# Scaling the softmax probabilities on GpSimd instead of VectorE, in both attentions of a two-layer hybrid block

## The chip, the cores and the metric

The kernel runs on one core of one Trainium2 chip. The metric is the device time of one execution in microseconds (us). Five engines work side by side, each through its own instructions strictly in the order in which they were written down: TensorE (PE; its weight loads are shown apart as PEld), VectorE (DVE), ScalarE (ACT), GpSimd (POOL) and SyncE (SP), which here only issues the transfers.

## The reference, cut to what matters

Two layers (`DEPTH = 2`), each over 256 tokens x and 256 context tokens of width 1024. Each layer has three branches (neighbourhood attention "NA", a gated spatial MLP, and latent attention "MLA"), gated and merged, then a squared-ReLU MLP. Only layer 0 also updates the context. Both attentions have 8 heads, and both end in the same softmax:

```
s = einsum(q, k) * scale          # NA: + bias, masked to a window
p = softmax(s, axis=-1)
y = einsum(p, v)
```

Queries of x attend to all 512 tokens; queries of the context (layer 0 alone) attend to the 256 context tokens.

## The kernel before, in words

Every projection is written as three matmuls per 128-row step (`mm3`, lines 287 to 289): a weight is split into a high part `wh` (ACT, line 115) and a remainder `wl` (DVE, line 116), and so are the activations.

Both attentions go through `soft_pv`. It takes a pair of heads at a time (`hh`) and 128 queries at a time (`qt`). For each head the steps are:

1. the score matmul into a PSUM tile `S` (tag "s", 2 buffers; line 410/411 in NA, line 417 in MLA)
2. in NA for queries of x, DVE adds the bias (line 443)
3. DVE takes the negated row maximum `nm` (line 445)
4. ACT writes `P = exp(S + nm)` to SBUF (tag "P", 2 buffers) and its row sum `sm` (line 448, two instructions)
5. DVE takes the reciprocal `r` (line 450)
6. DVE multiplies `P` by `r` in place (line 451)
7. PE turns `P` in blocks of 128x128 into a PSUM tile `pt` (tag "pt", **1 buffer**; line 454, four blocks for 512 keys, two for 256)
8. ACT copies `pt` to SBUF as `PT` (line 456)

When both heads and both `qt` are turned, PE multiplies `PT` by the values into `pv` (line 460). So a `pt` block can't start before ACT has copied the one before it, an exponential can't start before the `P` two heads earlier is turned, and a score can't start before the exponential two heads earlier has read its `S`.

While an attention runs, PE also has projection work that needs nothing of it: the gate and `z` matmuls of `merge` (lines 287 to 289). `paced` hands them out: each step of a projection may be issued only after a given score matmul (the `marks`). In layer 0 the projections work on 512 tokens, in layer 1 on 256. There are 96 heads' softmaxes in all: 32 in each attention of layer 0 (16 over 512 keys, 16 over 256) and 16 over 512 keys in each attention of layer 1.

The order of the instructions of each engine is not that of the source: the program is built with `schedule_with_timeline_sim=True`, a scheduler that lays out each engine's list ahead of time from its own estimates of durations. An edit to one operation can so move the others.

Of the kernel before, what the change touches and what calls it, by code (L numbers as in the profile page):

```python
# [10 lines left out]
ALU = mybir.AluOpType  # L11
# [15 lines left out]
def hybrid_block_kernel(tc, a, out):  # L27
    nc = tc.nc
    act = nc.scalar.activation
    vec = nc.vector  # L30
# [3 lines left out]
    with ExitStack() as es:  # L34
# [12 lines left out]
        def psum(tag, name):  # L47
            return pp.tile([128, 512], F32, tag=tag, name=name, bufs={"mm": 4, "s": 2, "pt": 1, "pv": 1}[tag])
# [378 lines left out]
        def soft_pv(score, V, pv, streams, bias, marks):  # L427

            for v in range(streams):
                kts = [0, 1, 2, 3] if v == 0 else [2, 3]  # L430
                k0, nk = kts[0] * 128, 128 * len(kts)
                PT = [gp.tile([128, 4, NX], F32, tag="PT", name="PT", bufs=2) for _ in range(2)]
                for qt in range(2):
                    q0 = v * NX + qt * 128
                    S = []
                    for hh in range(2):
                        s = psum("s", "S")
                        marks.append(score[hh](s[:, :nk], q0, k0, nk).ins)
                        S.append(s)
                    for hh in range(2):  # L440
                        s = S[hh]
                        if bias is not None and v == 0:
                            vec.tensor_tensor(out=s[:, :NX], in0=s[:, :NX], in1=bias[hh][:, qt, :], op=ALU.add)
                        nm = sp.tile([128, 1], F32, tag="nm", name="nm")
                        vec.tensor_reduce(out=nm, in_=s[:, :nk], axis=AX.X, op=ALU.max, negate=True)
                        P = gp.tile([128, 512], F32, tag="P", name="P", bufs=2)
                        sm = sp.tile([128, 1], F32, tag="sm", name="sm")
                        act(out=P[:, :nk], in_=s[:, :nk], func=AF.Exp, bias=nm, accum_out=sm)
                        r = sp.tile([128, 1], F32, tag="r", name="r")
                        vec.reciprocal(r, sm)  # L450
                        vec.tensor_scalar(out=P[:, :nk], in0=P[:, :nk], scalar1=r, scalar2=None, op0=ALU.mult)
                        pt = psum("pt", "pt")
                        for i in range(len(kts)):
                            nc.tensor.transpose(pt[:, i * 128:(i + 1) * 128], P[:, i * 128:(i + 1) * 128], ident)  # L454
                        n = len(kts)
                        turned = act(out=PT[hh][:, :n, qt * 128:(qt + 1) * 128],
                                     in_=pt[:, :nk].rearrange("p (i q) -> p i q", i=n), func=AF.Copy)
                for i, kt in enumerate(kts):
                    for hh in range(2):
                        m = mm(pv[64 * hh:64 * hh + 64, v * NX:(v + 1) * NX], lhsT=V[kt][hh], rhs=PT[hh][:, i, :],  # L460
                               start=(i == 0), stop=(i == len(kts) - 1), tile_position=(0, 64 * hh))
                        if i == 0 and hh == 0:

                            tc.add_manual_dep(m.ins, turned.ins.name, mybir.DependencyInfo(
                                mybir.DependencyClass.Sync, mybir.DependencyReason.DATA), reason="both heads")
# [68 lines left out]
        for l in range(L):  # L534
# [114 lines left out]
            for t in range(4):  # L649
                vec.tensor_scalar(out=cnat[t][:, 0:128], in0=cnat[t][:, 0:128], scalar1=rsc[:, t:t + 1], scalar2=None,  # L650
                                  op0=ALU.mult)
                if t in tts:
                    vec.tensor_scalar(out=cnat[t][:, 160:416], in0=cnat[t][:, 160:416], scalar1=rsc[:, 4 + t:5 + t],
                                      scalar2=None, op0=ALU.mult)
# [72 lines left out]
            for j in range(4):  # L727
                bias = []
                for hh in range(2):
                    bt = gp.tile([128, 2, NX], F32, tag="bias", name="bias", bufs=2)  # L730
                    with tc.issue_after(last_load[0]):
                        nc.sync.dma_start(out=bt, in_=a["nab"][l, 2 * j + hh])
                    bias.append(bt)
                pv = psum("pv", "pv")
                soft_pv([na_score(kT, qT, 2 * j + hh) for hh in range(2)],
                        [[vna[t][:, (2 * j + hh) * 64:(2 * j + hh + 1) * 64] for hh in range(2)] for t in range(4)],
                        pv, ns, bias, marks)
                H, Lo = split_out(pv, "yna", T)
                ynH.append(H)
                ynL.append(Lo)  # L740
# [86 lines left out]
            for j in range(4):  # L827
                pv = psum("pv", "pvm")
                soft_pv([mla_score(kmT, qmT, 2 * j + hh) for hh in range(2)],
                        [[vml[t][:, (2 * j + hh) * 64:(2 * j + hh + 1) * 64] for hh in range(2)] for t in range(4)],  # L830
                        pv, ns, None, marks)
                H, Lo = split_out(pv, "yml", T)
                ymH.append(H)
                ymL.append(Lo)
# [44 lines left out]
            for n in range(both, 8):  # L879
                out_chunk(a["wa"][l, 28 + n], n, mixH, mixL, [0], 16, acc)  # L880
                if last:
# [3 lines left out]
                                             op0=ALU.mult, op1=ALU.subtract)  # L885
# [165 lines left out]
```

## Time and profile before

| what | value |
|---|---|
| median of 3 runs | 1401.68 us (1401.63 to 1404.64) |
| the profiled execution | 1406.83 us, span 1404.8 us |
| PE busy | 1375.1 us (98% of the span) |
| PEld busy | 1165.9 us (83%) |
| DVE busy | 958.2 us (68%) |
| ACT busy | 703.5 us (50%) |
| POOL busy | 58.7 us (4%), 35 instructions |
| mean granted TensorE clock | 0.996 |

Busy time is the sum of an engine's instructions; a matmul's end is modelled, so a busy PE may still be waiting inside a row. The times of rows are counted from the start of the span. The profiled execution's own time is 5.15 us over the median of the runs.

### The profile page before, as it was taken

Reading aid. Unit: us, or ns where it says so; the run is one execution under the profiler, and the core shown is the slowest. Engines: PE = TensorE matmul, PEld = TensorE weight load, DVE = VectorE, ACT = ScalarE, POOL = GpSimd, SP = SyncE. Lnnn points to the kernel's source line nnn. Section 1 sums busy time; section 2 is a strip of 40 time slices with the busy share of each in tenths; the row PEclk is TensorE's granted clock in tenths of the full one; section 3 lists DMA queues with packets and bytes.
Section 4 is the critical chain, followed back from the end, with each engine's and each line's share of the span. In section 5 each row is a group of like instructions: output and inputs, shape, how many; then the busy total and the mean of one; then the engine's idle time right before and its main releaser. Section 6 shows DMA issues by size and latency. Waiting matters only on the chain.

```text
span 1404.8 us, 22573 instructions
## 1 busy us (share of the span) xinstructions
PE 1375.1 (98%) x8438; PEld 1165.9 (83%) x8438; DVE 958.2 (68%) x2071; ACT 703.5 (50%) x1440; POOL 58.7 (4%) x35
## 2 busy tenths in 40 slices
PE   6999999999999999999999999999999999999999
PEld 4888767777677789988888888988878879999998
DVE  4666477665563558899766665786778766877775
ACT  3466256444453346623324233566666665656654
POOL 0110000110000000000000000011003000000000
PEclk9999999999999999999999999999999999999999
DMA  9423542233313455765555552443533425666554
GB/s 335 144 84 105 181 143 90 74 106 120 120 45 106 135 189 169 211 206 173 195 199 192 181 193 90 149 137 94 180 106 110 124 78 166 192 181 177 184 182 149
DMA packets 67213, 210.61 MB, mean 150 GB/s; under 512 B 8608, under 2 KB 9632, under 8 KB 67104
## 3 DMA queue, kind: packets, MB, share of 16 engines
q1 hardware_dynamic: 67104, 209.18, 46.8%
q8 instruction: 66, 1.08, 0.3%
q14 instruction: 43, 0.35, 0.1%
HBM read 208.10 MB, written 1.05 MB: 149 GB/s over the span
## 4 chain that ended last, share of the span: by engine, by line
PE 96%; DVE 2%; ACT 1%; DMA 1%; issue 0%; SPq 0%; POOL 0%; ACTq 0%; DVEq 0%
PE o_ps L287 8%; PE o_ps L289 8%; PE o_ps L288 8%; PE f L288 6%; PE f L289 6%; PE f L287 6%; PE gate L287 5%; PE gate L288 5%; PE gate L289 5%; PE b_ps L287 5%; PE b_ps L288 4%; PE b_ps L289 4%; PE pt L454 3%; PE S L417 2%; PE z L287 2%; PE z L288 2%
## 5 line engine op out<-in xcount | busy, mean ns | idle before, releaser
L115 ACT ACTIVATE wh<-raw 128x512 fp32r<-128x512 f32 (+2 forms) x570 | 352.9, 626 | 517.4 <-PE o_ps L288 189.1
L116 DVE TENSOR_TENSOR wl<-raw,wh 128x512 fp32r<-128x512 f32 (+2 forms) x570 | 386.2, 685 | 185.0 <-ACT wh L115 180.2
L289 PE MATMUL f<-hH,wl 128*128 128x258 f32 (+2 forms) x560 | 180.7, 323 | 0.1
L287 PE MATMUL f<-hH,wh 128*128 128x258 f32 (+2 forms) x560 | 180.2, 323 | 0.5 <-ACT wh L115 0.5
L288 PE MATMUL f<-hL,wh 128*128 128x258 f32 (+2 forms) x560 | 180.3, 323 | 0.2 <-DVE hL L277 0.2
L288 PE MATMUL o_ps<-aL,wh 128*128 128x256 f32 (+1 forms) x544 | 176.0, 327 | 0.0
L287 PE MATMUL o_ps<-aH,wh 128*128 128x256 f32 (+1 forms) x544 | 175.8, 328 | 0.0
L289 PE MATMUL o_ps<-aH,wl 128*128 128x256 f32 (+1 forms) x544 | 175.4, 327 | 0.0
L287 PE MATMUL gate<-hH,wh 128*128 128x512 f32 (+1 forms) x384 | 140.9, 367 | 0.0
L289 PE MATMUL gate<-hH,wl 128*128 128x512 f32 (+1 forms) x384 | 131.4, 342 | 0.0
L288 PE MATMUL gate<-hL,wh 128*128 128x512 f32 (+1 forms) x384 | 131.1, 341 | 0.0
L287 PEld LDWEIGHTS f<-hH,wh 128*128 128x128 f32 x560 | 105.9, 190 | 9.0 <-ACT wh L115 0.7
L289 PEld LDWEIGHTS f<-hH,wl 128*128 128x128 f32 x560 | 106.1, 190 | 8.4 <-DVE wl L116 0.3
L288 PEld LDWEIGHTS f<-hL,wh 128*128 128x128 f32 x560 | 105.8, 190 | 8.7 <-DVE hL L277 0.4
L287 PEld LDWEIGHTS o_ps<-aH,wh 128*128 128x128 f32 x544 | 102.7, 190 | 9.4 <-ACT aH L918 0.8
L288 PEld LDWEIGHTS o_ps<-aL,wh 128*128 128x128 f32 x544 | 103.0, 190 | 8.7
L289 PEld LDWEIGHTS o_ps<-aH,wl 128*128 128x128 f32 x544 | 102.7, 190 | 8.8
L288 PE MATMUL b_ps<-wl,hH 128*128 128x512 f32 (+2 forms) x288 | 108.6, 380 | 0.0
L289 PE MATMUL b_ps<-wh,hL 128*128 128x512 f32 (+2 forms) x288 | 106.2, 380 | 0.0
L287 PE MATMUL b_ps<-wh,hH 128*128 128x512 f32 (+2 forms) x288 | 103.6, 385 | 0.0
L200 DVE SCALAR_TENSOR_TENSOR macc<-rawx,sS,macc 128x512 f32<-128x512 f32 x112 | 79.1, 750 | 28.8 <-DMA rawx<-in_wmod_dram 28.8
L287 PEld LDWEIGHTS gate<-hH,wh 128*128 128x128 f32 x384 | 73.6, 192 | 15.9 <-issue 7.5
(226 smaller groups left out, 2490.1 us busy)
## 6 DMA issues: line engine op xcount, KB each, us to landing
raw<-in_wa_dram SPq DMA_DIRECT2D x147, 512.0 KB, 3.6
raw<-in_w_dram SPq DMA_DIRECT2D x68, 512.0 KB, 3.6
raw<-in_wb_dram SPq DMA_DIRECT2D x32, 512.0 KB, 3.3
raw<-in_wmod_dram SPq DMA_DIRECT2D x32, 512.0 KB, 3.4
rawx<-in_wmod_dram SPq DMA_DIRECT2D x32, 512.0 KB, 4.5
raw<-in_wo_dram SPq DMA_DIRECT2D x24, 512.0 KB, 3.5
rawm<-in_wmod_dram SPq DMA_DIRECT2D x32, 256.0 KB, 6.0
rawx<-in_wmod_dram SPq DMA_DIRECT2D x32, 256.0 KB, 4.1
```

The source lines that it names most:

```text
L115: act(out=wh[:, :width], in_=src, func=AF.Copy)
L116: vec.tensor_tensor(out=wl[:, :width], in0=src, in1=wh[:, :width], op=ALU.subtract)
L200: summed = vec.scalar_tensor_tensor(out=o, in0=src, scalar=s, in1=o, op0=ALU.mult, op1=ALU.add)
L287: mm(ps, lhsT=sh, rhs=mh, start=first, stop=False)
L288: mm(ps, lhsT=sh, rhs=ml, start=False, stop=False)
L289: mm(ps, lhsT=sl, rhs=mh, start=False, stop=last)
L417: return mm(s, lhsT=Q[h][0:96, q0:q0 + 128], rhs=K[h][0:96, k0:k0 + nk], start=True, stop=True)
L454: nc.tensor.transpose(pt[:, i * 128:(i + 1) * 128], P[:, i * 128:(i + 1) * 128], ident)
```

## The change

The multiplication of `P` by `r` (line 451) is issued on GpSimd instead of VectorE. `soft_pv` serves both attentions, so all 96 of these move.

```
-                        vec.tensor_scalar(out=P[:, :nk], in0=P[:, :nk], scalar1=r, scalar2=None, op0=ALU.mult)
+                        nc.gpsimd.tensor_scalar(out=P[:, :nk], in0=P[:, :nk], scalar1=r, scalar2=None, op0=ALU.mult)
```

The scheduler then lays the lists out anew. On POOL the 96 rows stand between the reciprocal square roots (`rsh`) that were there alone. Near the end of layer 0's NA (`ssk` is a sum of squares of the keys that MLA needs):

```order
 L329 TENSOR_TENSOR rsh_2702<-ssk_2699,mhalf_86 128x8
+L451 TENSOR_SCALAR P_2393<-P_2393,r_2396 128x256
 L329 TENSOR_TENSOR rsh_2725<-ssk_2722,mhalf_86 128x8
```

The last of the 32 scalings of this attention now stands behind one such root.

On PE the transpositions move. In layer 1's NA (`P_10171` and `P_10186` are the two heads of one `qt`; `S_10219` and `S_10252` are scores of later ones):

```order
 L288 MATMUL gate_10515<-hL_8398,wh_10509 128x256
 L289 MATMUL gate_10515<-hH_8390,wl_10510 128x256
-L454 MATMUL pt_10177<-ident_79,P_10171 128x128 x4
 L410 MATMUL S_10219<-naK_9465,naQ_9244 128x512
 L411 MATMUL S_10219<-naK_9465,naQL2_9245 128x512
...
 L288 MATMUL z_10542<-yg_10006,wh_10543 128x256
 L289 MATMUL z_10542<-yg_10006,wl_10544 128x256
+L454 MATMUL pt_10177<-ident_79,P_10171 128x128 x4
 L454 MATMUL pt_10192<-ident_79,P_10186 128x128 x4
 L410 MATMUL S_10252<-naK_9462,naQ_9244 128x512
```

Where a score and two steps of `z` (six rows, of which the middle is left out) stood between the two heads' transpositions, the two now stand side by side, with nothing between them.

The same in layer 1's MLA, with a score and four steps of `gate` between the two before:

```order
 L288 MATMUL gate_11693<-hL_8393,wh_11683 128x256
 L289 MATMUL gate_11693<-hH_8385,wl_11684 128x256
-L454 MATMUL pt_11170<-ident_79,P_11164 128x128 x4
 L417 MATMUL S_11222<-kml_10854,qml_11114 128x512
 L287 MATMUL gate_11693<-hH_8386,wh_11683 128x256
...
 L289 MATMUL gate_11693<-hH_8389,wl_11688 128x256
+L454 MATMUL pt_11170<-ident_79,P_11164 128x128 x4
 L454 MATMUL pt_11188<-ident_79,P_11182 128x128 x4
 L417 MATMUL S_11224<-kml_10862,qml_11119 128x512
```

Here too the two transpositions become neighbours. Counted over the whole PE list, such neighbours (a transposition of one head right behind that of another) are:

| attention | before: 512 keys / 256 keys | after: 512 keys / 256 keys |
|---|---|---|
| NA, layer 0 | 1 / 0 | 6 / 2 |
| MLA, layer 0 | 0 / 0 | 4 / 4 |
| NA, layer 1 | 3 / 0 | 7 / 0 |
| MLA, layer 1 | 0 / 0 | 3 / 0 |

One of the three of layer 1 before, and two of the four over 256 keys in MLA of layer 0 after, have one matmul of a projection between the two. The list of SP, which issues the transfers, is the same as before.

## Rows read from the trace of the kernel before

**Rows 1.** The page: busy time of each engine, then the chain that ended last.
```profile
PE 1375.1 (98%) x8438; PEld 1165.9 (83%) x8438; DVE 958.2 (68%) x2071; ACT 703.5 (50%) x1440; POOL 58.7 (4%) x35
...
PE 96%; DVE 2%; ACT 1%; DMA 1%; issue 0%; SPq 0%; POOL 0%; ACTq 0%; DVEq 0%
```
**Rows 2.** Stretches of NA, MLA (layer 0), NA, MLA (layer 1): busy by engine, PEclk, DMA.
```profile
180.00:256.00 76.00, 73.40 (x429) 52.05 (x428) 55.48 (x146) 47.86 (x122) 0.18 (x1) 0.98 0.32 100
334.00:456.00 122.00, 122.00 (x645) 85.47 (x644) 61.86 (x148) 55.06 (x133) 0.00 (x0) 1.00 0.30 95
1013.00:1063.00 50.00, 43.92 (x289) 34.89 (x288) 36.55 (x90) 31.72 (x73) 0.00 (x0) 0.97 0.34 102
1107.00:1168.00 61.00, 60.91 (x430) 49.66 (x430) 38.10 (x82) 36.20 (x81) 0.00 (x0) 1.00 0.29 89
```
**Rows 3.** Steps of the softmax over all 96 heads: ns min/median/max.
```profile
L451 DVE TENSOR_SCALAR P<-P,r x96: 344/480/489, 186.6 to 1158.2; 128x512 f32<-128x512 f32 x64, 128x256 f32<-128x256 f32 x32
L448 ACT ACTIVATE P<-S,nm x96: 467/682/697, 185.6 to 1157.2; 128x512 f32<-128x512 f32 x64, 128x256 f32<-128x256 f32 x32
L456 ACT ACTIVATE PT<-pt x96: 364/597/602, 189.5 to 1163.6; 128x512 f32<-128x512 f32 x64, 128x256 f32<-128x256 f32 x32
```
**Rows 4.** Who waited for a tile P, in total: us, times.
```profile
  PE pt L454: 0.2, 1
```
**Rows 5.** Timeline of PE's weight loads, NA of layer 1: start us, us, ..., [wait before].
```profile
1032.59 0.46 PEld L454 LDWEIGHTS pt<-ident,P 128*128 128x128 f32 x4
1034.04 0.42 PEld L454 LDWEIGHTS pt<-ident,P 128*128 128x128 f32 x4 [0.98 <-ACT PT L456]
1034.70 0.19 PEld L410 LDWEIGHTS S<-naK,naQ 128*128 128x128 f32 x1 [0.25 <-ACT P L448]
...
1036.24 0.46 PEld L454 LDWEIGHTS pt<-ident,P 128*128 128x128 f32 x4
1036.66 0.19 PEld L410 LDWEIGHTS S<-naK,naQ 128*128 128x128 f32 x1
```
**Rows 6.** The same view at two other neighbouring pairs of before (NA).
```profile
209.04 0.59 PEld L454 LDWEIGHTS pt<-ident,P 128*128 128x128 f32 x4
210.61 0.42 PEld L454 LDWEIGHTS pt<-ident,P 128*128 128x128 f32 x4 [0.98 <-ACT PT L456]
211.27 0.19 PEld L410 LDWEIGHTS S<-naK,naQ 128*128 128x128 f32 x1 [0.25 <-ACT P L448]
...
1044.64 0.42 PEld L454 LDWEIGHTS pt<-ident,P 128*128 128x128 f32 x4 [0.82 <-ACT PT L456]
```
**Rows 7.** Timeline of ACT and DVE: the softmax of the head turned at 1036.24.
```profile
1034.45 0.20 ACT L448 ACTIVATION_READ_ACCUMULATOR P<-S,nm 128x1 f32 x1
...
1034.69 0.16 DVE L450 RECIPROCAL r<-sm 128x1 f32<-128x1 f32 x1 [0.67 <-ACT P L448]
1034.96 0.49 DVE L451 TENSOR_SCALAR P<-P,r 128x512 f32<-128x512 f32 x1
```
**Rows 8.** POOL's instructions by form: busy us, mean ns of one.
```profile
L329 POOL TENSOR_TENSOR rsh<-ssk,mhalf 128x8 f32<-128x8 f32 x8 | 14.1, 1784 | 180.1 <-DVE ssk L765 180.1
...
masks.py:199 POOL TENSOR_SCALAR_AFFINE_SELECT ident<-ident 128x128 f32<-128x128 f32 x1 | 0.3, 292 | 0.1
masks.py:197 POOL MEMSET ident<- 128x128 f32 x1 | 0.2, 204 | 0.3 <-POOLq L1040 0.3
...
L1040 POOL MEMSET const-float32-1.0<- 128x1 f32 x1 | 0.1, 98 | 0.0
```
**Rows 9.** Waits of PE's weight loads in NA of layer 1 (1013 to 1063): us, times, longest.
```profile
PEld S L410 <- ACT P L448: 3.4, 5, 1.3
PEld pt L454 <- ACT PT L456: 2.7, 3, 1.0
```
**Rows 10.** A stretch of NA of layer 1 after an idle time of PE; columns as in rows 2.
```profile
1018.60:1021.70 3.10, 3.10 (x15) 3.00 (x14) 2.92 (x7) 1.38 (x4) 0.00 (x0) 0.52 0.27 52
```
**Rows 11.** DVE's remainder `wl` over the whole run: ns min/median/max.
```profile
L116 DVE TENSOR_TENSOR wl<-raw,wh x570: 549/691/715, 20.0 to 1396.2; 128x512 fp32r<-128x512 f32 x182, 128x416 fp32r<-128x416 f32 x6, 128x384 fp32r<-128x384 f32 x2
```

## The prediction
> **What bounds the kernel now.** Read first the page's busy shares and the chain of waits: PE is busy for 98% of the span and carries 96% of the chain that ended last, DVE 2%, ACT 1%, POOL nothing [rows 1]. Whatever doesn't make PE stand still, or spare it a standstill, is worth nothing; DVE, from which the work is taken, is at 68%. Then read the four stretches in which the attentions run [rows 2]. In MLA of layer 0 PE has no idle time (122.00 of 122.00 us), in MLA of layer 1 almost none (60.91 of 61), in NA of layer 0 2.6 us and in NA of layer 1 6.1 us. So the softmax hides behind the projections' matmuls except in NA, and there the waits show what ends last: PE waits for ACT's exponential to give a score tile back (3.4 us) and for ACT's copy to give `pt` back (2.7 us) [rows 9]. For the scaling itself PE waited 0.2 us, once, in the whole run [rows 4]. That one number says that there is nothing to win on the line that is edited.
>
> **Part 1, what leaves DVE.** 64 scalings of 512 columns at 0.48 us and 32 of 256 at 0.344 [rows 3]: 64 x 0.48 + 32 x 0.344 = 41.7 us of DVE. All of it lies beside PE's work [rows 1, 4]. Worth 0.
>
> **Part 2, what POOL gets.** No row of before shows a multiplication on POOL, so it is bounded by its neighbours [rows 8]. Below: filling 128 columns takes 204 ns and one column 98, that is 0.83 ns per column, so 512 columns take 0.53 us. Above: the select over 128 columns takes 292 ns, which over the same 98 ns is 1.53 ns per column, so 0.88 us. [...] I take the upper end, 0.88 (0.49 for 256 columns), as the select reads a tile like the scaling does. The 96 scalings are then 64 x 0.88 + 32 x 0.49 = 72 us on an engine that was busy for 58.7 [rows 1].
>
> Is the longer way to `P` covered? Take the head whose exponential ends at 1034.65 and which is turned at 1036.24 [rows 5, 7]. DVE was done with it at 1035.45, so 0.79 us were to spare. On POOL the scaling takes 0.40 us more and hands over twice between engines; one such step costs some 0.2 us by the row, since ACT's sum ends at 1034.65 and the scaling, after a reciprocal of 0.16 and its own wait, starts at 1034.96. 0.40 + 0.2 is less than 0.79: covered, with the order as it was. In the new order this very head (`P_10171`) is turned a score and two steps of `z` later. Those two things took from 1034.70 to 1036.24 less one step of three matmuls (0.35), 1.2 us. So POOL may take up to about 0.79 + 0.48 + 1.2 - 0.2 = 2.3 us before PE waits for it. Cost 0. Where nothing follows to cover it, at the ends of the two NA stages, and where one root (1.78 us) now stands in front of the last scaling, I put 1.5 us on the path.
>
> **Part 3, what moves on PE.** This is the term that decides. `pt` has one buffer, so the second of two neighbouring transpositions can't start before ACT has copied the first. The rows of before have this case [rows 5]: the first starts at 1032.59, the second, after 0.98 us of waiting for the copy, at 1034.04, and the score behind it, after another 0.25 us for the exponential, at 1034.70: 2.11 us. A transposition that stands alone takes from 1036.24 to 1036.66, 0.42 us. The pair costs 2.11 - 2 x 0.42 = **1.27 us**, and since PE runs in order nothing can fill it. The other pairs agree: waits of 0.98 and 0.82 us, and 2.23 us from start to score for the one in layer 0 [rows 6].
>
> The order has 20 such pairs over 512 keys where it had 4: 16 x 1.27 = 20.3 us. It has 6 over 256 keys where it had none. No row shows one of those; the copy takes 0.364 us there where it takes 0.597 [rows 3], so 1.27 - 0.23 = 1.04, of which I take 1.0 as two of the six still have a matmul in between: 6.0 us. Bounds per pair: 0.82, the smallest wait seen, to 1.39 (2.23 - 0.84) for 512 keys; 0.6 (0.82 - 0.23) to 1.27 for 256.
>
> Against it: a pair does at once some of the waiting that single heads do now. Of the 6.1 us that PE waits in NA of layer 1 for a score tile and for `pt` [rows 9], 3.4 + 2.7, the three pairs of before hold at most 3 x (0.98 + 0.25) = 3.7, and the first score's wait stays; I take off 2 us there and 1.3 us in NA of layer 0. The MLA stages have no such wait to give back [rows 2]. Nothing else changes place: SP's list is the same.
>
> **Sum.** 0 + 0 + 1.5 + 20.3 + 6.0 - 3.3 = +24.5 us. The profiled execution took 1406.83 us and would take 1431.3. It lies 5.15 us over the median of the runs, and the terms are rows of the same kernel, so I put the sum on the median: 1401.68 + 24.5 = **1426.2 us**. Own ends: low 16 x 0.82 + 6 x 0.6 = 16.7, less 5 for waits given back: +12, or 1413.7. High 16 x 1.39 + 6 x 1.27 = 29.9, plus 3 for the ends of stages, plus a lower clock: after the idle time before 1018.6 the granted clock was 0.52 for 3.1 us [rows 10], the lower of its two levels (1.2 GHz), which loses half of 3.1, some 1.6 us; five such more are 8: +41, or 1443. After the pairs of before no fall shows, so the sum has none.
>
> **Rivals.**
> *Faster.* The scaling leaves DVE's list, where it queues behind other work, so `P` could be ready earlier, and the waits for ACT in NA shrink with it. If all that PE waits in NA of layer 1 for score tiles and `pt` went [rows 9], that is 6 us, 1395.6. It decides only if a neighbouring pair costs under about 0.2 us, so that 22 of them stay under 4 us; all rows of pairs show 0.8 us and more, and PE hardly waited for the scaling [rows 4]. 4%.
> *No change.* The pairs' waits stand where PE would have waited anyway. That holds for NA at best; in the MLA stages PE is busy to the end [rows 2]. To bring all of the 24.5 us within the 4.2 us (0.3%) that a measurement can tell from no change, the MLA pairs would have to cost nothing. 5%.
> *Late scaling.* POOL takes over 2.3 us for 512 columns, and PE waits for `P`. For it: POOL's one arithmetic row costs 1.78 us for 8 columns [rows 8], and DVE works on SBUF all the while, `wl` at 0.69 us a piece [rows 11]. Against it: fill and select run at about 1 ns per column. With 3 us each full scaling is 0.7 us late: 64 x 0.7 = 45 on top of 24.5, 1471. 10%.
> The Trainium skill, page "SBUF — State Buffer", section "Who interferes with whom", states that VectorE instructions with two SBUF inputs and GpSimd instructions that read SBUF hold a shared port pair exclusively, and whichever comes second waits for the whole of the other. `wl` has two SBUF inputs. By that rule a scaling could wait out one `wl`: 0.88 + 0.69 = 1.57 us, still under 2.3, so the sum by it stays +24.5; no run here shows it yet.
> That the change doesn't do what it says is out: 96 rows leave DVE's list and 96 come into POOL's.
>
> **How the numbers follow.** 81% for the forecast, 10% for the late scaling, 5% for no change, 4% for faster. Slower by over 0.3%: 81 + 10 = 91%; within 0.3%: 5%; faster: 4%. The range takes the forecast's own ends, goes on below to where two thirds of the sum are given back elsewhere (+8) and above into the milder late scalings (half of that rival's 45 us on top): 1409 to 1449.
>
> **What would show it.** Right: PE's idle time in the four stretches grows by some 20 us in all; waits of `pt` for ACT's copy rise from 5 us or less in the NA stages to about 20, some 0.9 each; DVE loses 42 us; POOL shows 96 scalings under 1 us, and PE hardly waits for `P`. Wrong: pairs with waits of under 0.4 us; PE waiting for POOL; scalings of over 2 us; a lower granted clock that lasts through a stage.

## The result, and the profile after

The changed kernel takes **1438.97 us** (median of 4 runs, 1438.4 to 1440.74), the kernel before beside it on the same chip 1401.66 us: the medians lie **37.3 us** apart, and by all runs together it takes 1.0259 times as long [1.0244, 1.0275]. The forecast was +24.5 us, in a range of +7 to +47. The profiled execution of after took 1438.53 us.

The page of after, the lines that answer to [rows 1]:

```profile
PE 1381.6 (96%) x8438; PEld 1163.0 (81%) x8438; DVE 928.7 (65%) x1975; ACT 704.7 (49%) x1440; POOL 188.6 (13%) x131
...
PE 93%; ACT 2%; DVE 2%; DMA 1%; issue 1%; SPq 0%; POOL 0%; ACTq 0%; DVEq 0%; POOLq 0%
```

DVE lost 96 instructions and 29.5 us, POOL got 96 and 129.9 us. The chain still runs through PE, but ACT now holds 2% of it: PE stands and waits for ACT more than it did.

Where the time went is read from the four stretches in which the attentions run, each from its first score matmul to that of the next, or to POOL's next root behind it. The columns are those of [rows 2]. The kernel before first, in a second profiled execution (why the second, is told under the last experiment):

```profile
182.32:333.18 150.86, 145.47 (x814) 108.88 (x813) 100.48 (x241) 80.15 (x190) 13.64 (x8) 1.00 0.33 104
333.18:537.84 204.66, 204.34 (x1097) 154.85 (x1096) 110.79 (x236) 90.32 (x196) 0.00 (x1) 1.00 0.39 124
1011.40:1105.43 94.03, 87.03 (x625) 76.18 (x623) 74.52 (x177) 62.37 (x139) 13.98 (x6) 0.98 0.40 125
1105.43:1219.46 114.03, 113.99 (x868) 102.29 (x868) 80.15 (x184) 68.52 (x148) 0.00 (x1) 1.00 0.41 131
```

And after:

```profile
180.45:347.35 166.90, 150.61 (x815) 109.96 (x813) 91.88 (x210) 81.95 (x193) 54.41 (x40) 0.99 0.31 94
347.35:560.78 213.43, 207.30 (x1097) 155.46 (x1096) 100.48 (x204) 90.37 (x196) 39.96 (x33) 1.00 0.38 118
1034.35:1133.60 99.25, 88.06 (x624) 75.44 (x622) 69.77 (x161) 61.78 (x139) 37.15 (x22) 0.98 0.38 117
1133.60:1252.96 119.36, 115.83 (x868) 102.42 (x868) 75.60 (x168) 68.67 (x148) 26.17 (x16) 1.00 0.40 125
```

The length of a stretch is its second number, PE's busy time the third. NA of layer 0 is 16.0 us longer, MLA 8.8, NA of layer 1 5.2, MLA 5.3: together 35.4 us of the rows unrounded, and what lies between and behind the stretches has not changed. What lies in front of the first is 1.9 us shorter here (180.45 against 182.32 us), and it differs between the two profiled executions of before as well (181.04 in the first). PE's idle time in the four stretches (length less busy) rose from 5.4 + 0.3 + 7.0 + 0.0 = 12.7 us to 16.3 + 6.1 + 11.2 + 3.5 = 37.1, by 24.4.

What PE waited for over the whole run of after (us, times, longest; PEld are its weight loads, "issue" names nobody):

```profile
PEld pt L454 <- issue: 23.7, 34, 1.0
PE pt L454 <- ACT PT L456: 19.5, 27, 1.0
...
PEld pt L454 <- POOL P L451: 11.0, 12, 1.6
...
PEld S L410 <- ACT P L448: 8.8, 22, 1.4
...
PE pt L454 <- POOL P L451: 2.5, 2, 1.3
```

The same wait for the copy in the second execution of before:

```profile
PE pt L454 <- ACT PT L456: 2.8, 4, 0.7
```

The copy that gives `pt` back costs PE 19.5 us, where it was 2.8 in four waits before. And PE now waits for POOL's scaling, which before was 0.2 us, once [rows 4]. One neighbouring pair in MLA of layer 1 of after, where before PE had no idle time (the timeline of PE, its weight loads and ACT, columns as in [rows 5]):

```profile
1145.17 0.46 PEld L454 LDWEIGHTS pt<-ident,P 128*128 128x128 f32 x4
1145.27 0.60 PE L454 MATMUL pt<-ident,P 128*128 128x128 f32 x4
...
1145.91 0.60 ACT L456 ACTIVATE PT<-pt 128x512 f32<-128x512 f32 x1 [0.93 <-PE pt L454]
...
1146.62 0.42 PEld L454 LDWEIGHTS pt<-ident,P 128*128 128x128 f32 x4 [0.99 <-issue]
1146.65 0.63 PE L454 MATMUL pt<-ident,P 128*128 128x128 f32 x4 [0.78 <-ACT PT L456]
...
1147.22 0.30 PEld L417 LDWEIGHTS S<-kml,qml 96*128 96x128 f32 x2 [0.19 <-ACT P L448]
```

The copy starts at 1145.91 and takes 0.60; only then, at 1146.62, does the second transposition begin. From the first weight load to the score behind the pair it is 2.05 us, 1.21 more than two transpositions that stand alone (0.42 each [rows 5]). That is the pair of [rows 5] over again, in a stage that had none.

The scaling on POOL itself, by form (busy us, mean ns of one, then the idle time before it):

```profile
L451 POOL TENSOR_SCALAR P<-P,r 128x512 f32<-128x512 f32 x64 | 102.2, 1602 | 218.8 <-DVE r L450 208.3 <-PE gate L288 5.0 <-PE mod_ps L137 2.1
L451 POOL TENSOR_SCALAR P<-P,r 128x256 f32<-128x256 f32 x32 | 30.1, 940 | 57.3 <-DVE r L450 46.6 <-PE pt L454 10.5
```

1.60 us where DVE needed 0.48, and 0.94 where it needed 0.344. The forecast had 0.88 and 0.49. From 256 to 512 columns it is 0.66 us more, 2.6 ns a column; the select of [rows 8], which the forecast took for the nearest row, gave 1.53.

### The profile page after: what moved, and what is told of

It is laid out like the page before. It is cut to its first block, busy times and chain, and to the rows that moved or that the text cites. A ratio compares the mean times of both kernels' runs of the same rounds, so it can differ in the third digit from the quotient of the medians.

```text
span 1436.7 us, 22752 instructions
## 1 busy us (share of the span) xinstructions
PE 1381.6 (96%) x8438; PEld 1163.0 (81%) x8438; DVE 928.7 (65%) x1975; ACT 704.7 (49%) x1440; POOL 188.6 (13%) x131
## 4 chain that ended last, share of the span: by engine, by line
PE 93%; ACT 2%; DVE 2%; DMA 1%; issue 1%; SPq 0%; POOL 0%; ACTq 0%; DVEq 0%; POOLq 0%
PE o_ps L287 8%; PE o_ps L289 8%; PE o_ps L288 8%; PE f L288 6%; PE f L287 6%; PE f L289 6%; PE gate L287 5%; PE gate L288 4%; PE gate L289 4%; PE b_ps L287 4%; PE b_ps L289 4%; PE b_ps L288 4%; PE pt L454 3%; PE S L417 3%; PE z L287 2%; PE z L288 2%
## 5 line engine op out<-in xcount | busy, mean ns | idle before, releaser
L116 DVE TENSOR_TENSOR wl<-raw,wh 128x512 fp32r<-128x512 f32 (+2 forms) x570 | 390.2, 691 | 190.6 <-ACT wh L115 183.4
L451 POOL TENSOR_SCALAR P<-P,r 128x512 f32<-128x512 f32 (+1 forms) x96 | 132.3, 1381 | 276.1 <-DVE r L450 254.9
```

The lines of the kernel that those rows point to most:

```text
L116: vec.tensor_tensor(out=wl[:, :width], in0=src, in1=wh[:, :width], op=ALU.subtract)
L451: nc.gpsimd.tensor_scalar(out=P[:, :nk], in0=P[:, :nk], scalar1=r, scalar2=None, op0=ALU.mult)
```

## The experiments

**Pairs without POOL.** The kernel before, scaling on DVE, with one new wait: the first head's transposition over 512 keys waits until the second head is scaled too. So the two stand side by side: 23 neighbouring pairs over 512 keys, where before has three with nothing between them.

```
-    vec.tensor_scalar(out=P[:, :nk], ...)
+    scaled = vec.tensor_scalar(out=P[:, :nk], ...)
+    Ps.append((P, scaled))
+for hh in range(2):
     ...
     tr = nc.tensor.transpose(pt[...], P[...], ident)
+    if hh == 0 and i == 0 and v == 0:
+        tc.add_manual_dep(tr.ins, Ps[1][1].ins.name, ...)
```

> The scaling stays on VectorE; each first transposition over 512 keys is made to wait for the second head's scaling, so that the two stand side by side: 23 neighbouring pairs over 512 keys (3 before), none over 256. Theory A (the pairs' wait for the single pt buffer is the cost, 1.27 us each): +25 us, about 1427. Theory B (the cost is POOL's 1.60 us a scaling, and pairs hardly matter): 1402 to 1410.

Measured: 1434.77 us, 1.0234 times before [1.0215, 1.0253], +32 us. Its waits:

```profile
PE pt L458 <- ACT PT L463: 19.1, 27, 1.7
...
PE pt L458 <- DVE P L452: 2.1, 2, 1.9
```

27 waits of PE for the copy, 19.1 us, against 27 and 19.5 in after. In MLA of layer 1, at the same granted clock as before, the stretch lasts 121.57 us where it lasted 114.03:

```profile
1127.13:1248.70 121.57, 117.19 (x868) 102.61 (x868) 81.75 (x184) 69.07 (x148) 0.00 (x1) 1.00 0.39 123
```

The order alone, with POOL left out, costs nearly as much as the change did, and more than the 25 us of theory A. Some of it is the new wait's own, since the first head is held back for the second (PE waits 2.1 us for the scaling, where it was 0.2), and some the granted clock, whose mean was 0.995 in all four executions and 0.998 to 1.0 in the seven of before beside them. So this run shows that pairs are dear, not what the change's pairs cost to the tenth.

**POOL without pairs.** The changed kernel, with a rule of order only: a score is queued on PE behind the transposition of the head three before it. The list then has one neighbouring pair; all 96 scalings stay on POOL.

```
+turns = []
...
-    marks.append(score[hh](s[:, :nk], q0, k0, nk).ins)
+    sc = score[hh](s[:, :nk], q0, k0, nk).ins
+    if len(marks) >= 3:
+        tc.add_manual_dep(sc, turns[len(marks) - 3], ...NoSync...)
+    marks.append(sc)
...
+    turns.append(tr.ins.name)
```

> The scaling runs on POOL as in the change, but each score is queued on PE behind the transposition three heads earlier, so that the transpositions stand apart as before (1 pair left). Theory A (pairs): only the ends of the stages are left, +3 to +8 us, 1405 to 1410. Theory B (late P): with 1.60 us instead of 0.48 and one hand-over more, against 0.79 us to spare, each full scaling is some 0.5 us late: 64 x 0.5 = +32 us or more, 1434 and up.

Measured: 1414.03 us, 1.0085 [1.0064, 1.0105], by the medians 11.3 us over the 1402.78 of before beside it (the 11.9 of an expectation below comes from the ratio). That lies between the two theories, nearer to A: two thirds of the loss are gone with the pairs. Its four stretches:

```profile
181.84:341.28 159.44, 150.71 (x814) 110.25 (x813) 91.79 (x209) 80.67 (x191) 56.14 (x40) 0.98 0.31 99
341.28:545.85 204.57, 204.25 (x1097) 154.57 (x1096) 100.11 (x204) 90.28 (x196) 40.95 (x33) 1.00 0.38 124
1019.40:1114.80 95.40, 88.32 (x625) 75.61 (x623) 70.81 (x161) 61.81 (x139) 39.15 (x22) 0.98 0.39 123
1114.80:1228.80 114.00, 113.96 (x868) 102.26 (x869) 75.66 (x168) 68.72 (x148) 26.60 (x17) 1.00 0.41 131
```

Both MLA stages last as long as before to 0.1 us, with 48 scalings on POOL in them, which over the run took 1.65 and 0.97 us on average. What is left lies in NA. There, but for two waits of weight loads, PE waits for the scaling:

```profile
PEld pt L463 <- POOL P L460: 11.0, 17, 3.2
...
PE pt L463 <- POOL P L460: 5.3, 5, 2.8
```

The longest, 3.2 us for the weight load and 2.8 for PE, is the end of NA in layer 0, where the last scaling stands behind a root, as the forecast's first order block shows (its rows are in the section on the prediction).

The two kernels give a sum by stretch. From before to this one (POOL, no pairs): 8.6 - 0.1 + 1.4 + 0.0, or **9.8 us**. From this one to the changed kernel (the pairs): 7.5 + 8.9 + 3.8 + 5.4, or **25.5 us** (166.90 - 159.44 and so on). Together 35.4 (sums of the rows as they stand, rounded at the end). The second sum holds whatever else differs between the two lists. The first is not idle time alone: of the 8.6 us in NA of layer 0, PE's idle time makes 3.3 (8.73 against 5.39), and the granted clock, 0.98 where it was 1.00, some 3 more (an estimate, 0.02 x 159 us). The rest lies inside PE's rows.

**The same order on DVE**, and **MLA on POOL, NA on DVE.** Both have the rule of order of the last kernel. The first is the control for it; in the second the line reads `(vec if bias is not None else nc.gpsimd).tensor_scalar(...)`, and only NA has a bias.

> Scaling on DVE as before, transpositions forced apart as in e2_pool_apart (one neighbouring pair left, before has 4). Theory A (the neighbouring pairs carry most of the change's cost; the POOL scaling adds the rest where it comes late): no new pairs and no late P, so within 5 us of before; the three pairs of before that go are worth about 1.3 us each, so likeliest 1398 to 1402 us. Theory B (the time comes with the POOL scaling itself, and the order does not matter): also before's time, 1400 to 1404. The forced order itself has a price (rival C): if e2_pool_apart's 11.9 us came from holding scores back and not from POOL, this kernel shows them too, 1412 or more, and PE waits for P or S as there.

> As e2b_dve_apart, but the 48 scalings of the two MLA attentions run on POOL. Theory A: in MLA the 1.6 us scaling is covered as long as the transpositions stand apart, so within 2 us of e2b_dve_apart, and the two MLA stages last 204.5 and 114 us. Theory B (a POOL scaling costs by itself, about 37/96 = 0.4 us each): 48 x 0.4 = 19 us more than e2b_dve_apart.

Measured: 1400.36 us, 0.9983 [0.9972, 0.9994], and 1402.19 us, 0.9993 [0.9981, 1.0005]. So the rule of order costs nothing, and what the kernel with POOL and no pairs loses comes from POOL. The NA stretches of the first are 1.1 and 1.9 us shorter than before's, at the same clock, with one neighbouring pair fewer in the one and two in the other, so about 1.0 us a pair:

```profile
181.69:331.42 149.73, 145.43 (x814) 108.66 (x813) 99.94 (x240) 79.81 (x189) 13.65 (x8) 1.00 0.33 105
...
1009.64:1101.77 92.13, 86.73 (x624) 75.45 (x622) 74.53 (x177) 62.05 (x139) 13.19 (x6) 0.98 0.40 127
```

And 48 of the 96 scalings on POOL cost 1.8 us by the medians, with intervals that overlap; 0.4 us each would have been 19. The MLA stages of the second:

```profile
332.33:536.91 204.58, 204.26 (x1097) 154.56 (x1096) 100.30 (x204) 90.40 (x196) 41.01 (x32) 1.00 0.39 123
...
1102.79:1217.24 114.45, 114.23 (x868) 102.33 (x869) 75.40 (x168) 68.37 (x148) 26.64 (x17) 1.00 0.41 131
```

With the transpositions apart, the place decides what the slower scaling costs: it is covered in MLA and not in NA. The version with all scalings on DVE is the one kernel here that comes out ahead of before, by 0.17%, too little to call a gain.

**Only 256 keys back on DVE.** The rule of order, POOL for all but the 16 scalings over 256 keys in NA of layer 0.

> As e2_pool_apart, but the 16 scalings of 256 columns in NA of layer 0 stay on DVE; the 80 others run on POOL. The trace of e2_pool_apart has PE waiting for P in NA of layer 0 with 256 keys (0.3 to 0.4 us each) and at its end, behind a root (one wait of over 3 us). If these heads carry what is left there, most of the 5.7 us of NA in layer 0 go: 1406 to 1410 us. If the 512-key heads carry it, it stays at 1412 to 1414.

Measured: 1411.27 us, 1.0057 [1.004, 1.0074], between the two expectations. NA of layer 0:

```profile
180.51:336.33 155.82, 148.45 (x814) 110.09 (x813) 95.40 (x224) 80.23 (x190) 39.37 (x24) 0.99 0.31 101
```

3.6 us less than with all on POOL, still 5.0 more than before. Some of both numbers is the granted clock. The times of the six executions go with it: two took 1407.4 and 1407.9 us at a mean clock of 0.998 and 0.999, four took 1411.1 to 1414.0 at 0.995 to 0.996. The profiled one (1412.02) is one of the four, and NA of layer 1, where the scalings are issued as in the kernel with POOL and no pairs (95.40 us at 0.98), took 97.98 in it at 0.95:

```profile
1014.47:1112.45 97.98, 90.68 (x625) 77.48 (x623) 70.80 (x161) 62.14 (x139) 41.63 (x22) 0.95 0.39 120
```

So how the heads share the loss to the tenth stays open. That the heads over 512 keys carry part of it shows in NA of layer 1, which has no others: with POOL and no pairs it lasts 1.4 us longer than before, at the same clock.

**Half a tile at a time.** An attempt at a remedy: `pt` used as two halves of 256 columns in turn, two blocks turned and copied at a time, so that ACT's copy could run beside the next two blocks. On DVE and on POOL.

```
-    pt = psum("pt", "pt")
-    for i in range(len(kts)):
-        nc.tensor.transpose(pt[:, i * 128:(i + 1) * 128], ...)
+    for i in range(0, len(kts), 2):
+        pt = next(rooms)
+        for d in range(2):
+            nc.tensor.transpose(pt[:, d * 128:(d + 1) * 128], ...)
```

> The kernel before (scaling on VectorE) with pt used in the same two halves: the control of the one above, and a possible gain. Theory A: the four pairs of before and some waits go, 1396 to 1402. Theory B: 1401 to 1404, nothing to win.

> The change, with pt used in two halves of two blocks each, each copied by itself, so that a transposition waits for a copy of half the length and only for the half it writes. Theory A (pairs wait for the copy): at least half of the pairs' cost goes, 1415 to 1425. Theory B (late P): 1434 to 1440, as the change.

Measured: 1461.49 us, 1.0423 [1.0398, 1.0447], and 1478.35 us, 1.0542 [1.0522, 1.0562]. It went backwards. PE's weight loads on DVE's version, one head of MLA:

```profile
1179.99 0.24 PEld L464 LDWEIGHTS pt<-ident,P 128*128 128x128 f32 x2
1180.94 0.20 PEld L464 LDWEIGHTS pt<-ident,P 128*128 128x128 f32 x2 [0.71 <-ACT PT L466]
```

The second half waits 0.71 us for the copy of the first, though it writes other columns: the wait was kept for the whole tile, and one head now holds inside it the stop that a pair had between two. With 47 waits of PE for the copy (24.0 us) instead of 4 the time rises, past every expectation. As a remedy it failed; as a dose of neighbours it points the way of the pairs.

**Before, profiled again.**

> The kernel before, profiled a second time. Its first profiled execution lay 5.2 us over the median of its runs. If that was an accident of that execution, this one comes at 1400 to 1404 us, and one of the stages shows where the 5 us were; if profiling itself costs it, again about 1406.

Measured: 1405.24 us, between the two expectations. That profiling costs the difference is not shown, since the profiled executions of the other kernels lie within 1.4 us of their medians (after 1438.53 and 1438.97, the same order on DVE 1401.70 and 1400.36). The stretches are those shown at the start. Among 23 executions of before that ran beside this one the times go from 1398.67 to 1407.35 us. The first profiled execution differs in NA of layer 0, which took 153.78 us there and 150.86 here; twice the granted clock fell in it (first block) and not here (second; the same two times of the span):

```profile
192.50:196.00 3.50, 3.50 (x14) 2.94 (x13) 1.95 (x5) 2.79 (x7) 0.00 (x0) 0.53 0.57 155
291.50:295.00 3.50, 3.32 (x9) 3.09 (x10) 3.41 (x12) 3.50 (x10) 0.00 (x0) 0.52 0.47 150
```

```profile
192.50:196.00 3.50, 3.50 (x26) 2.53 (x26) 1.74 (x6) 2.34 (x6) 0.00 (x0) 1.00 0.74 205
291.50:295.00 3.50, 3.42 (x16) 3.03 (x17) 3.41 (x12) 3.50 (x10) 0.00 (x0) 1.00 0.46 150
```

Each costs a little under half of 3.5 us, together some 3.3 us, about the 2.9 by which the stretch is longer. So NA of layer 0 is better compared with the second execution.

## Why the prediction was right, and where it was short

- **Direction and cause: right.** PE's idle time in the stretches rose by 24.4 us (some 20 forecast), its waits for the copy to 19.5 us in 27 waits of 0.7 on average (about 20, of 0.9), and the runs with and without pairs show that the order on PE carries the larger part. Two of the signs named for "wrong" came too, and belong to Part 2 below: PE waits for POOL (2.5 us in two waits), and two of the 96 scalings took over 2 us.
- **Part 1, DVE: right.** 41.7 us leave DVE. Its busy time falls by 29.5 only, since `wl` takes some 4 us more in all (390.2 against 386.2; last section), and since a row begins up to 0.1 us before the one ahead has ended, which busy time counts once. Nothing is won by either.
- **Part 3, the pairs: right, and near in size.** 20.3 + 6.0 - 3.3 = 23.0 us were forecast; the changed kernel less the same with the transpositions apart is 25.5, good to some 2 us, since the clock in NA of layer 0 was 0.99 in the one and 0.98 in the other. By stretch: MLA of layer 0 8.8 measured for 9.1; MLA of layer 1 5.3 for 3.8, where a fourth pair with four matmuls of projections in between (after's list, at 1170.32 and 1171.91) still waited 0.62 us and was not counted as one. The 3.4 and 2.7 us of [rows 9], from which what is given back was taken, are waits of weight loads; PE's own matmuls waited 2.2 and 2.1 us there, so that their sum equals PE's idle time of 6.1 is chance.
- **Part 2, POOL: this is the term that was mis-sized.** "I take the upper end, 0.88 (0.49 for 256 columns)" and "Cost 0 ... I put 1.5 us on the path." A scaling takes 1.60 us (0.94), nearly twice the upper bound, and POOL without pairs costs 9.8 us by the stretches (11.3 by the medians), all of it in NA. The bound was the wrong row: a select over 128 columns does not price a multiplication by a column of scalars.
- **The clock: put at nothing, and not nothing.** "After the pairs of before no fall shows, so the sum has none." The four executions of after have a mean granted clock of 0.996, the 23 of before under the last experiments one of 0.9986; by that some 4 us of the 37.3 are the clock's (an estimate, 0.0026 x 1439, and part of the two terms above, not on top of them).
- The allowance of 2.3 us was worked out for one head in NA of layer 1 and then used for all 96. It held in MLA, where 1.6 us cost nothing. In NA it did not: PE waits there for `P` itself, for a score tile that comes back later because `P` is late (5.2 us in 11 waits with POOL and no pairs, 2.2 in two before), and at the end of the stage. That end, in layer 0, on POOL and PE in after:

```profile
266.02 1.67 POOL L329 TENSOR_TENSOR rsh<-ssk,mhalf 128x8 f32<-128x8 f32 x1 [0.80 <-DVE ssk L765]
...
267.68 1.45 POOL L451 TENSOR_SCALAR P<-P,r 128x256 f32<-128x256 f32 x1
...
269.09 0.39 PE L780 MATMUL h_tr<-ident,knat 128*96 128x128 f32 x2 [1.91 <-DVE knat L770]
269.10 1.98 POOL L329 TENSOR_TENSOR rsh<-ssk,mhalf 128x8 f32<-128x8 f32 x1
...
269.32 0.38 PE L454 MATMUL pt<-ident,P 128*128 128x128 f32 x2
```

The root holds up the last scaling, as forecast, and the scaling holds up the next root (at 269.10), which was not forecast. But PE waits for neither here. Its 1.91 us, where it was 0.3 before, are for the keys of the first root, which had waited for DVE and not for a scaling; in the new list the transposition of these keys stands in front of that of the last `P`, where before it stood behind it. With POOL and no pairs the list has the old order, and there PE does wait for the last scaling:

```profile
258.40 1.67 POOL L329 TENSOR_TENSOR rsh<-ssk,mhalf 128x8 f32<-128x8 f32 x1 [1.89 <-DVE r L459]
...
260.05 2.00 POOL L460 TENSOR_SCALAR P<-P,r 128x256 f32<-128x256 f32 x1
...
262.10 0.69 PE L463 MATMUL pt<-ident,P 128*128 128x128 f32 x2 [2.76 <-POOL P L460]
```

The reciprocal for it was done at 258.37, so the root holds the scaling up by 1.7 us, and the scaling itself takes 2.00 us where the two before it took 0.92 and 0.93. The forecast had the first of these two, not the second.

- The rival *Late scaling* (POOL over 2.3 us for 512 columns) did not come: the longest of 96 took 2.19 in after (one took 2.46 with POOL and no pairs). But what it stands for, PE waiting for `P`, came below its point, for want of cover in NA. *No change* and *Faster* fell with the pairs.

Still open: how the 9.8 us divide between heads of 512 keys, heads of 256, the end of the stage and the granted clock; and why the scheduler put transpositions side by side. Its rules were not examined, only the lists that it wrote.

## What to carry to other kernels

When an operation changes its engine under a scheduler, compare the lists of the engine that bounds the kernel first: where two users of a buffer that exists once become neighbours, price the pair from one that the trace already has, and hold them apart with a rule of order (here worth 25 us of 37). Then check the cover of the slower operation stage by stage: the same 1.6 us were free in one attention and cost some 10 us in the other, part of them through the clock. For an operation without a row of its kind on the new engine, leave the range open upward by more than the nearest simple row says.

## What the runs showed of the hardware

**POOL and DVE slow each other, in part.** The remainder `wl` on DVE, over the whole run of after (ns min/median/max), against [rows 11]:

```profile
L116 DVE TENSOR_TENSOR wl<-raw,wh x570: 551/691/1141, 19.9 to 1428.1; 128x512 fp32r<-128x512 f32 x182, 128x416 fp32r<-128x416 f32 x6, 128x384 fp32r<-128x384 f32 x2
```

The median has not moved, the longest went from 0.715 to 1.141 us. Two of them, beside a scaling:

```profile
1039.68 1.57 POOL L451 TENSOR_SCALAR P<-P,r 128x512 f32<-128x512 f32 x1 [17.23 <-DVE r L450]
...
1039.84 1.07 DVE L116 TENSOR_TENSOR wl<-raw,wh 128x512 fp32r<-128x512 f32 x1
...
1041.50 1.56 POOL L451 TENSOR_SCALAR P<-P,r 128x512 f32<-128x512 f32 x1 [0.26 <-DVE r L450]
...
1041.89 0.84 DVE L116 TENSOR_TENSOR wl<-raw,wh 128x512 fp32r<-128x512 f32 x1
```

Each `wl` lies within a scaling for its whole length, took 0.38 and 0.15 us longer than its 0.69, and the scalings kept their 1.56. The Trainium skill, page "SBUF — State Buffer", section "Who interferes with whom", calls the ports that the two share an exclusive lock; by that rule the second would wait for the whole of the first, and the first `wl` would have ended 0.69 us after the scaling, 2.10 us from its start (an estimate). The trace agrees that they interfere, not that they exclude each other. It goes the other way too: six of the 64 scalings over 512 columns in after took 1.85 to 2.19 us instead of 1.56, each with a `wl` beside it. In MLA, where 48 scalings run, nothing of it reached PE. At the end of NA it did: the scaling of 2.00 us shown in the section on the prediction had a `wl` and both products for the keys on DVE beside it.

**A wait on PE can cost twice.** In the kernel with POOL and no pairs, PE stood 2.8 us for the last scaling of NA in layer 0, and the granted clock fell to the lower of its two levels (1.2 of 2.4 GHz) there; its mean over the 7 us is 0.53:

```profile
261.00:268.00 7.00, 5.85 (x20) 3.78 (x21) 4.70 (x11) 3.28 (x8) 2.68 (x2) 0.53 0.01 2
```

That is 0.47 x 7 = 3.3 us lost to the clock, of which the wait itself hides a part. The lower clock was no accident of that execution: the mean clock was 0.995 to 0.996 in all four of this kernel, 0.998 to 1.0 in the seven of before beside them and in the twelve with the same order on DVE. Of the 11.3 us some 5 are then the clock's (an estimate, 0.0036 x 1414). And a single fall is not certain: the two executions of before have the same wait of 1.7 us for a transfer in front of 192.5, and only in one of them did the clock fall behind it. The two falls of that one run are 0.2% of its time.
